# Split weights stored and reloaded through GpSimd's DMA queue in a hybrid decoder step

## The chip, the cores and the metric

One core of a Trainium2 chip runs the whole kernel. The metric is the device time of one launch in microseconds, the median of several runs. The engines are PE (TensorE, matrix products; PEld are its weight loads), DVE (VectorE), ACT (ScalarE), POOL (GpSimd) and SP (SyncE, which here only issues DMA transfers).

## The reference

One layer of a decoder, applied to a prompt of 1024 tokens and to 8 single new tokens with states of their own. Everything is float32, the width D is 1024.

```python
p = jnp.einsum('btd,dn->btn', x, w_in)                  # N_IN = 9360 columns
p_gla, p_rwkv, p_gate = _split(p, (GLA_COLS, RWKV_COLS, GATE_COLS))
# branch 1: gated linear attention, 4 heads, chunked scan over a 128x256 state
o_gla, S_gla = _gla_chunked(q, k, v, log_a, S_gla0)
# branch 2: RWKV-7, 16 heads of 64, token shift, per-token recurrence on a 64x64 state
y, S_rwkv = _rwkv7_scan(rh, w, kh, vh, kk, a, S_rwkv0)
...
m = sigmoid(gate_a) * (o_gla @ w_up_gla) + sigmoid(gate_b) * (o_rwkv @ w_up_rwkv)
y_out = _layernorm(DEEPNORM_ALPHA * x + m @ w_out, ln_g, ln_b, LN_EPS)
```

The outputs are y for both groups, and the new states and shift rows.

## The kernel before, in words

**Tiling and passes.** The tokens are handled in two passes (`PASS`): the first has 512 prompt tokens and the 8 samples (tiles of 256 and 264 columns), the second the other 512 prompt tokens (one tile of 512 columns). In each pass the input projection runs block by block: a block is 128 columns of `w_in` against all 1024 rows, that is 8 steps of 128. When both passes are through the projection, a tail does the two up-projections, the merge, `w_out` and the layer norm.

**Split operands.** For accuracy each float32 operand of the large products is split in a high part, rounded to the format that PE takes at full speed (fp32r), and a low part, the remainder. A product is three matrix products: high x high, high x low, low x high. For a half block of weights (four steps, 128x512) the first pass loads the raw weights into a buffer `wraw` (3 of them), ACT casts the high part into a buffer `wpart` (5 of them, each 128x2x512), and DVE or POOL subtracts to make the low part. The whole `wpart`, 512 KB, is then stored to a scratch tensor `w` in DRAM, `kept[c0, j]`. The second pass needs the same weights: it makes no new split, but loads each stored `wpart` back. There are 73 blocks of `w_in` with two halves each: 146 stores and 146 loads. A buffer `wpart` comes free when PE has done its last product with it. The tail's weights `w_up_gla` and `w_up_rwkv` are split anew, without a store.

**The order of the work.** The kernel's order is not left to a compiler. A planner (class `Order`, method `run`) holds a set of streams, each a generator that yields one operation after the other. At every step it takes, over all streams, the operation that could start first by its own reckoning, corrected by priorities (`PRIO`, `ON_PE`), and emits it. The emitted order is the order of each engine's queue, so what stands first in a queue and waits holds up what stands behind it. To reckon a start the planner keeps `time` for each engine, `ready` and `read` for each tile, `dma` for the time at which the DMA queue will have moved what it was given, and prices from `price` (engine and size) and `transfer` (time in the DMA engines, and a lag until landing). The object `E` stands for operations that DVE or POOL may do (`C` for ACT or DVE): `start` then takes the engine that ends first, with `ASIDE` 0.5 us added where POOL would share its way to memory with DVE.

**Queues.** In the kernel before, every DMA is issued by SP, through one queue. One price holds for each, 0.56 us.

All instructions that the planner emits are recorded at one helper line, L217; tiles tell them apart. `w<-wpart` is a store, `wpart<-w` a load, `wraw<-w_in` a load of raw weights. `proj`, `big`, `pch` and `pY` are PSUM banks, `row`, `wide`, `X`, `XT`, `rh` working tiles, `sg` gate rows kept in DRAM, `XD` and `LD` scratch tensors in DRAM by which small blocks are laid out anew.

Of the kernel before, what the change touches and what calls it, by code (L numbers as in the profile page):

```python
# [10 lines left out]
F32 = mybir.dt.float32  # L11
# [10 lines left out]
D = 1024  # L22
# [107 lines left out]
class Op:  # L130


    def __init__(self, ways, out, ins, lag=0.0, table=None, tiles=None, port=""):
        self.ways, self.out, self.ins, self.lag, self.table, self.tiles = ways, out, ins, lag, table, tiles
        self.port, self.outs = port, [out]
        self.eng, self.fn, self.cost = ways[0]


# [6 lines left out]
def price(eng, name, out, args, ins):  # L145

    n = out.free_size()
    src = [x for x in ins if x.tensor.space != PSUM] if eng == "A" else ins
    if eng == "P":
        m = args[0].free_size()  # L150
        rows, cols = tiles(name, args)
        if name == "transpose":
            return 0.112 * rows / P
        if args[0].dtype == F32R:
            return max(m / 1200, n / 2165)
        if rows == cols == P:
            return 2 * max(m, n) / 1200 + 0.005
        return 2 * (max(m, n) if cols == P else m + n) / 1200 * min(0.5 if cols == P else 0.25, rows * cols / P ** 2) + (0.01 if cols == P else 0.0)
    if eng == "S":
        return 0.56  # L160
    if eng == "A":
        extra = len(ins) - 1
        return 0.097 + n / 1200 + (0.042 if len(src) == len(ins) else 0.0) + 0.094 * extra
    wide = max([n, *(x.free_size() for x in ins)]) if name in ("tensor_reduce", "bn_stats", "bn_aggr") else n
    if eng == "V":
        if name == "tensor_tensor_scan":
            return 0.1 + n / 480
        if name in ("tensor_copy", "copy", "memset") and ins and ins[0].tensor.space != PSUM:
            wide = wide / 2
        scalars = sum(x.free_size() == 1 for x in ins[1:]) if name in ("scalar_tensor_tensor", "tensor_scalar") else 0  # L170
        return 0.068 + wide / (480 if name == "copy_predicated" else 960) + 0.06 * scalars
    if name in ("tensor_scalar", "memset"):
        return 0.08 + n / 760
    return 0.1 + n / (300 if name == "tensor_copy" else 456)
# [31 lines left out]
class Engine:  # L206
# [3 lines left out]
    def __getattr__(self, name):  # L210
        def make(out, *args, **kw):
            ins = [x for x in (*args, *kw.values()) if isinstance(x, AP)]
            ways = []
            lag, table, part, port = 0.0, None, None, ""
            for eng, handle in self._handles.items():
                call = getattr(handle, "tensor_copy" if (eng, name) == ("V", "copy") else name)
                ways.append((eng, lambda call=call: call(out, *args, **kw), price(eng, name, out, args, ins)))  # L217
                if eng in "VG" and shared(eng, name, out, ins):
                    port += eng
            if eng == "S":  # L220
                lag = transfer(out, args[0])
            elif eng == "A" and name == "activation":
                table = SETS.get(args[1])
            elif eng == "P":
                part = tiles(name, args)
            return Op(ways, out, ins, lag, table, part, port)
        return make


# [26 lines left out]
class Order:  # L256
# [4 lines left out]
    def __init__(self, nc):  # L261
        self.P, self.A, self.V, self.G, self.S, self.E, self.C = (Engine(**e) for e in (
            {"P": nc.tensor}, {"A": nc.scalar}, {"V": nc.vector}, {"G": nc.gpsimd}, {"S": nc.sync},
            {"V": nc.vector, "G": nc.gpsimd}, {"A": nc.scalar, "V": nc.vector}))
        self.tiles = (P, P)
        self.quads = {"V": {}, "A": {}}
        self.time = dict.fromkeys("PAVGS", 0.0)
        self.port = dict.fromkeys("VG", 0.0)
        self.dma = 0.0
        self.table = EXP  # L270
        self.ready, self.read = {}, {}
        self.streams = []
        self.idle, self.make, self.home, self.wait = {}, {}, {}, {}
        self.kept, self.tile = {}, {}
# [65 lines left out]
    def start(self, op):  # L340

        best = None
        for eng, fn, cost in op.ways:
            free, t = self.time[eng] + (SWITCH if eng == "P" and op.tiles != self.tiles else 0.0), 0.0
            for x in (*op.outs, *op.ins):
                at, by = self.ready.get(x.tensor.name, (0.0, None))
                if eng == "S" and by == "D" and x is op.out:
                    continue
                if by != eng:
                    at += HOP.get(by, 0.0) + (SPARE if eng == "P" and by in ("V", "A", "G") else LANDED if by == "D" else 0.0)  # L350
                elif eng != "P" and x is not op.out:
                    at += 0.13
                t = max(t, at)
            t = max(t, *(self.read.get(x.tensor.name, 0.0) for x in op.outs))
            if eng in op.port:
                free = max(free, self.port["G" if eng == "V" else "V"])
            late, t = free - t, max(t, free)
            if eng in "VA" and self.held(eng, op):
                cost += HOLD
            end = t + cost  # L360
            if len(op.ways) > 1:
                end += BIAS if eng == "V" and "A" in op.ways[0][0] else ASIDE if eng == "G" and "G" in op.port else 0.0
            if best is None or end < best[0]:
                best = end, t
                op.eng, op.fn, op.cost, op.late = eng, fn, cost, max(0.0, late)
        return best[1]
# [10 lines left out]
    def run(self):  # L377
        while self.streams:
            best, before = None, list(self.streams)
            self.urgent = self.needed()  # L380
            for s in before:
                self.advance(s)
                if s.op is not None:
                    t = self.start(s.op)
                    key = t - (s.on_pe + SWITCH * (s.op.tiles != self.tiles) if s.op.eng == "P" else s.prio)
                    if s.kind in self.urgent:
                        key -= URGENT
                    if s.op.table not in (None, self.table):
                        key += max(0.0, TABLE - AGE * s.op.late)
                    if best is None or key < best[0]:  # L390
                        best = key, t, s
            if best is None:
                assert self.streams != before, "streams wait for one another"
                continue
            _, t, s = best
            op, s.op = s.op, None
            cost = op.cost
            if op.table not in (None, self.table):
                cost += TABLE
                self.table = op.table  # L400
                self.nc.scalar.preload_act_table_set(self.table)  # L401
            op.fn()
            self.time[op.eng] = max(self.time[op.eng], t + cost)
            if op.eng in op.port:
                self.port[op.eng] = t + cost
            if op.eng == "P":
                self.tiles = op.tiles
            elif op.eng in "VA":
                for x, q in self.starts(op):
                    self.quads[op.eng][x is op.out, x.space] = q  # L410
            end = t + cost
            if op.eng == "S":
                self.dma = max(self.dma, end) + op.lag[0]
                end = self.dma + op.lag[1]
            for x in op.outs:
                n = x.tensor.name
                self.ready[n] = max(end, self.ready.get(n, (0.0,))[0]), "D" if op.eng == "S" else op.eng
            for x in op.ins:
                n = x.tensor.name
                self.read[n] = max(self.read.get(n, 0.0), end)  # L420


class Kern(Order):
# [224 lines left out]
    def load_w(self):  # L648
# [16 lines left out]
        def low():  # L665
            for n in range(count):
# [4 lines left out]
                self.free(raw)  # L671
                if src is self.a["w_in"] and i == 0:
                    kept[c0, j] = self.dr.tile([P, 2, 512], F32, name=f"w{c0}_{j}")
                    yield self.S.dma_start(kept[c0, j], w.bitcast(F32))
                self.ws.append(w)
                los.append(w)
            self.w_done = True
# [3 lines left out]
        for n, (src, c0, j, i) in enumerate(todo):  # L681
            if src is self.a["w_in"] and i:
                yield lambda: len(los) == len(raws)
                w = yield from self.get("wpart")
                yield self.S.dma_start(w.bitcast(F32), kept[c0, j])
                self.ws.append(w)
                continue
            raw = yield from self.get("wraw")
# [1151 lines left out]
```

## Time and profile before

| | |
|---|---|
| median of 3 runs | 1487.62 us (1485.31 to 1491.81) |
| the profiled execution's own time | 1487.92 us |
| its span in the profile | 1486.1 us |
| granted TensorE clock, mean | 0.996 |
| PE busy | 1449.8 us (98%) |
| DVE, ACT busy | 1194.8 us (80%), 857.7 us (58%) |
| POOL busy, instructions | 113.6 us (8%), 208 |
| moved by DMA | 318.96 MB, mean 215 GB/s |

The span runs from the first to the last instruction of the kernel; the time of the execution is 1.8 us longer. Busy times leave out the issuing of DMAs. Windows count from the start of the span. In lists of waits a row has the engine and tile that waited, what ended the wait, the total in us, the number of waits and the longest. The first store goes out at 9.1 us and the last at 568.0; the loads run from 568.5 to 1160.2 us.

### The profile page before, as it was taken

The numbers are of one execution on the slowest core, as the hardware profiler recorded it, in microseconds if no ns is written. First come the engines' busy times: TensorE is split into PE (matmuls) and PEld (weight loads), VectorE is DVE, ScalarE is ACT, GpSimd is POOL, SyncE is SP. The second block draws the span as 40 slices with busy tenths as digits, with TensorE's granted clock in tenths as the row PEclk, the third lists the DMA queues.
The fourth block names the chain that finished last, engine by engine and source line by source line (L and its number), as shares of the span: only waits on it lengthen the run. The fifth ranks groups of instructions, "written<-read, shape, count | busy, mean of one in ns | idle before, by whom it ended". The sixth has DMA issues, their size and how long they took to land. (4 is left out here: it accounts for less than half of the span.)

```text
span 1486.1 us, 31563 instructions
## 1 busy us (share of the span) xinstructions
PE 1449.8 (98%) x11158; PEld 1260.4 (85%) x11158; DVE 1194.8 (80%) x3255; ACT 857.7 (58%) x2196; POOL 113.6 (8%) x208
## 2 busy tenths in 40 slices
PE   9999999999999999999999999999999999999997
PEld 6998999899989998787777777878787898988786
DVE  6697889888998899879878989898877866755665
ACT  5666776676767776665754555474547645544210
POOL 1001010201010102000101020111001000000000
PEclk9999999999999999999999999999999999999999
DMA  8886786678676877566566556656564766888432
GB/s 299 273 285 202 250 296 214 226 253 295 202 258 211 294 229 258 170 224 188 160 198 179 155 190 191 192 154 188 174 189 138 229 210 221 295 293 271 139 107 85
DMA packets 211258, 318.96 MB, mean 215 GB/s; under 512 B 91811, under 2 KB 107180, under 8 KB 211100
## 3 DMA queue, kind: packets, MB, share of 16 engines
q1 hardware_dynamic: 211100, 316.93, 66.8%
q8 instruction: 89, 1.46, 0.4%
q14 instruction: 69, 0.57, 0.1%
HBM read 197.19 MB, written 118.61 MB: 212 GB/s over the span
## 5 line engine op out<-in xcount | busy, mean ns | idle before, releaser
L217 PE MATMUL proj<-xs,wpart 128*128 128x264 f32 (+2 forms) x5640 | 1017.7, 327 | 1.4 <-DVE row L217 0.8
L217 PEld LDWEIGHTS proj<-xs,wpart 128*128 128x128 f32 x5640 | 808.5, 189 | 80.3 <-issue 9.9
L217 ACT CAST wpart<-wraw 128x512 fp32r<-128x512 f32 x210 | 130.2, 623 | 103.5 <-PE proj L217 49.6
L217 DVE TENSOR_TENSOR row<-row 128x512 f32<-128x512 f32 (+7 forms) x321 | 166.3, 524 | 12.4 <-ACT row L217 5.6
L217 DVE TENSOR_TENSOR wpart<-wraw,wpart 128x512 fp32r<-128x512 f32 x207 | 145.2, 702 | 32.3 <-ACT wpart L217 31.4
L217 ACT ACTIVATE row<-row 128x512 f32<-128x512 f32 (+5 forms) x213 | 128.8, 610 | 14.4 <-DMA row<-sg 6.5
L217 POOL TENSOR_TENSOR row<-row 128x512 f32<-128x512 f32 (+5 forms) x64 | 72.7, 1143 | 746.3 <-DVE row L217 396.4
L217 DVE TENSOR_TENSOR Xt<-X,wide 128x60 f32<-128x60 f32 (+24 forms) x496 | 104.8, 211 | 11.7 <-DMA wide<-LD 1.8
L217 DVE TENSOR_TENSOR X<-X,Xt 128x60 f32<-128x60 f32 (+24 forms) x496 | 105.4, 213 | 10.0
L217 ACT ACTIVATE row<-proj,omu 128x256 f32<-128x256 f32 (+1 forms) x99 | 54.0, 546 | 93.5 <-PE proj L217 93.3
L217 PE MATMUL big<-xs,wpart 128*128 128x256 f32 (+2 forms) x576 | 101.7, 332 | 0.0
L217 PEld LDWEIGHTS big<-xs,wpart 128*128 128x128 f32 x576 | 87.7, 194 | 9.7 <-issue 0.2
L217 DVE SCALAR_TENSOR_TENSOR wide<-pch,pc,s0p 64x64 f32<-64x64 f32 x208 | 58.7, 282 | 32.9 <-PE pch L217 28.0
L217 ACT COPY row<-wide 64x64 f32<-64x64 f32 x240 | 57.9, 241 | 40.2 <-DVE wide L217 34.7
L401 ACT ACT_TABLE_LOAD x62 | 79.5, 1283 | 1.1
L217 DVE SCALAR_TENSOR_TENSOR row<-proj,pv,row 128x255 f32<-128x255 f32 (+1 forms) x99 | 56.3, 569 | 22.4 <-ACT tail L217 13.7
L217 PE MATMUL big<-row 128*32 128x32 f32 (+4 forms) x936 | 65.3, 241 | 1.4 <-ACT row L217 1.4
L217 ACT COPY row<-big 128x128 f32<-128x128 f32 (+6 forms) x134 | 38.7, 318 | 42.2 <-PE big L217 36.7
L217 ACT COPY wide<-pch 64x64 f32<-64x64 f32 x159 | 32.8, 206 | 47.0 <-PE pch L217 45.1
L217 ACT ACTIVATE row<-proj 128x128 f32<-128x128 f32 (+4 forms) x136 | 36.9, 324 | 37.4 <-PE proj L217 37.0
L217 PE MATMUL pch<-wide,gg 128*128 128x128 f32 x256 | 51.6, 283 | 5.5 <-DVE wide L217 4.7
L217 PEld LDWEIGHTS pch<-wide,gg 128*128 128x128 f32 x256 | 42.3, 189 | 16.1 <-PE proj L217 4.7
(249 smaller groups left out, 1992.6 us busy)
## 6 DMA issues: line engine op xcount, KB each, us to landing
w<-wpart SPq DMA_DIRECT2D x146, 512.0 KB
wpart<-w SPq DMA_DIRECT2D x146, 512.0 KB
wraw<-w_in SPq DMA_DIRECT2D x146, 256.0 KB
wide<-LD SPq DMA_DIRECT2D x64, 128.0 KB
wraw<-w_up_gla SPq DMA_DIRECT2D x32, 256.0 KB
wraw<-w_up_rwkv SPq DMA_DIRECT2D x32, 256.0 KB
sg<-row SPq DMA_DIRECT2D x16, 260.0 KB
row<-sg SPq DMA_DIRECT2D x16, 260.0 KB
```

The source lines that it names most:

```text
L217: ways.append((eng, lambda call=call: call(out, *args, **kw), price(eng, name, out, args, ins)))
L401: self.nc.scalar.preload_act_table_set(self.table)
```

## The change

The stores of `wpart` in the first pass and its loads in the second are issued by POOL (`self.G.dma_start`) instead of SP (`self.S.dma_start`). All other DMAs stay on SP. The planner is told: a DMA on POOL has the price 1.2 us and 1.0 us more until it lands, `dma` is kept for each of the two queues, and what it had tied to the engine SP (`eng == "S"`) is now tied to the operation being a DMA (`op.moves`). As the planner reckons with other prices and two queues, the order that it emits changes on every engine.

```diff
-        self.port, self.outs = port, [out]
+        self.port, self.outs, self.moves = port, [out], False
...
-    if eng == "S":
-        return 0.56
+    if name == "dma_start":
+        return 0.56 if eng == "S" else 1.2
...
-                if eng in "VG" and shared(eng, name, out, ins):
+                if eng in "VG" and name != "dma_start" and shared(eng, name, out, ins):
                     port += eng
-            if eng == "S":
+            if name == "dma_start":
                 lag = transfer(out, args[0])
...
-        self.dma = 0.0
+        self.dma = dict.fromkeys("SG", 0.0)
...
-                if eng == "S" and by == "D" and x is op.out:
+                if op.moves and by == "D" and x is op.out:
                     continue
...
-            if op.eng == "S":
-                self.dma = max(self.dma, end) + op.lag[0]
-                end = self.dma + op.lag[1]
+            if op.moves:
+                self.dma[op.eng] = max(self.dma[op.eng], end) + op.lag[0]
+                end = self.dma[op.eng] + op.lag[1] + (1.0 if op.eng == "G" else 0.0)
...
                     kept[c0, j] = self.dr.tile([P, 2, 512], F32, name=f"w{c0}_{j}")
-                    yield self.S.dma_start(kept[c0, j], w.bitcast(F32))
+                    yield self.G.dma_start(kept[c0, j], w.bitcast(F32))
...
                 w = yield from self.get("wpart")
-                yield self.S.dma_start(w.bitcast(F32), kept[c0, j])
+                yield self.G.dma_start(w.bitcast(F32), kept[c0, j])
```

More of the change, by code (lines that the diff above doesn't have):

```diff
@@ L225, in make @@
                 part = tiles(name, args)
-            return Op(ways, out, ins, lag, table, part, port)
+            op = Op(ways, out, ins, lag, table, part, port)
+            op.moves = name == "dma_start"
+            return op
         return make
@@ L411, in run @@
             end = t + cost
-            if op.eng == "S":
-                self.dma = max(self.dma, end) + op.lag[0]
-                end = self.dma + op.lag[1]
+            if op.moves:
+                self.dma[op.eng] = max(self.dma[op.eng], end) + op.lag[0]
+                end = self.dma[op.eng] + op.lag[1] + (1.0 if op.eng == "G" else 0.0)
             for x in op.outs:
                 n = x.tensor.name
-                self.ready[n] = max(end, self.ready.get(n, (0.0,))[0]), "D" if op.eng == "S" else op.eng
+                self.ready[n] = max(end, self.ready.get(n, (0.0,))[0]), "D" if op.moves else op.eng
             for x in op.ins:
```

## Prediction

> **What bounds the kernel now.** I read the page first (busy shares, then the chain that ended last), then the stages by window, then the lists of waits, and last the rows of the tiles that the change touches.
>
> ```profile
> span 1486.1 us, 31563 instructions
> ...
> PE 1449.8 (98%) x11158; PEld 1260.4 (85%) x11158; DVE 1194.8 (80%) x3255; ACT 857.7 (58%) x2196; POOL 113.6 (8%) x208
> ...
> PE 27%; DMA 2%; DVE 1%; issue 0%; ACT 0%; POOL 0%; SPq 0%; POOLq 0%; DVEq 0%
> ```
>
> PE is busy 1449.8 us of 1486.1, so at most 36.3 us of open idle time can be won without taking work off PE, and the change takes none off. The queues of SP and POOL have 0% of the chain. Some of the 36.3 us is the two ends: the first matmul waits 1.7 us for a memset (row below), and the last stretch of PE in the chain ends at 1475.61 + 2.86 = 1478.5 us, 7.6 us before the end. About 27 us lie between.
>
> ```profile
> 1475.61 2.86 PE big L217 x24
> ```
>
> The stages, with columns span, PE, PEld, DVE, ACT, POOL, granted clock, DMA share and GB/s:
>
> ```profile
> 100.00:200.00 100.00, 96.99 (x886) 90.80 (x886) 82.97 (x238) 67.91 (x188) 6.16 (x12) 1.00 0.75 239
> 200.00:300.00 100.00, 98.23 (x960) 95.16 (x957) 86.49 (x262) 67.98 (x197) 11.71 (x25) 1.00 0.72 234
> 300.00:400.00 100.00, 98.99 (x934) 95.10 (x934) 86.75 (x253) 69.67 (x200) 7.11 (x13) 1.00 0.79 262
> 400.00:500.00 100.00, 96.69 (x962) 91.34 (x960) 90.20 (x245) 72.78 (x197) 12.61 (x26) 1.00 0.73 238
> 500.00:600.00 100.00, 97.96 (x926) 91.25 (x925) 89.44 (x260) 69.46 (x189) 10.10 (x16) 1.00 0.74 243
> 600.00:700.00 100.00, 99.55 (x707) 78.53 (x706) 86.77 (x271) 59.30 (x152) 3.36 (x11) 1.00 0.64 198
> 700.00:800.00 100.00, 97.02 (x628) 77.62 (x627) 79.23 (x214) 59.68 (x145) 12.23 (x20) 1.00 0.58 176
> 800.00:900.00 100.00, 97.09 (x712) 78.39 (x711) 88.76 (x272) 55.18 (x140) 14.60 (x19) 1.00 0.57 175
> 900.00:1000.00 100.00, 98.52 (x671) 77.99 (x670) 89.88 (x251) 58.19 (x143) 15.71 (x22) 1.00 0.61 185
> 1000.00:1100.00 100.00, 99.16 (x608) 80.36 (x606) 79.86 (x226) 51.70 (x139) 8.26 (x18) 1.00 0.63 182
> ```
>
> The reader is to see that PE is near its limit in both passes, that DVE is next with 80 to 90% (86 on the mean of these ten), that the DMA engines have room (0.57 to 0.79), and that POOL is nearly empty. What PE still waits for is DVE above all, and a DMA only once by name:
>
> ```profile
> PEld pch L217 <- DVE rh L217: 6.8, 10, 2.3
> ```
> ```profile
> PE pch L217 <- DVE wide L217: 6.0, 9, 1.7
> PE pch L217 <- DVE rh L217: 4.1, 4, 1.8
> ...
> PE big L217 <- POOL XT L562: 1.7, 1, 1.7
> ...
> PE big L217 <- DMA X<-XD: 1.2, 1, 1.2
> ```
>
> **The change, part by part.** It moves 292 transfers of 512 KB: 146 stores w<-wpart in the first pass and 146 loads wpart<-w in the second. Nothing is removed or added.
>
> ```profile
> L217 SPq DMA_DIRECT2D w<-wpart x146: 319/433/1667, 9.1 to 568.0; - x146
> L217 SPq DMA_DIRECT2D wpart<-w x146: 319/325/597, 568.5 to 1160.2; - x146
> ```
>
> *SP is relieved.* 146 x 0.433 + 146 x 0.325 = 110.7 us of issuing leave it, and with them the waits at its head:
>
> ```profile
> SPq L217 <- PE proj L217: 216.6, 93, 6.9
> ```
>
> This is SP between 570 and 1160 us, where a load waits for PE to be done with a weight buffer, 93 times and 2.3 us on the mean; what is queued behind it waits too. Who gains: the small transfers that others wait for.
>
> ```profile
> DVE X L217 <- DMA XT<-XD: 4.3, 6, 1.3
> ```
> ```profile
> ACT wpart L217 <- DMA wraw<-w_in: 8.7, 8, 2.1
> ACT row L217 <- DMA row<-sg: 6.5, 5, 2.4
> ```
>
> These are engines with idle time of their own, and PE itself waits 1.2 us for a transfer. So the direct gain lies between 0 and the 27 us that PE idles at all; I take 1.5 us, near the 1.2 of PE's own row.
>
> *POOL issues 292 transfers.* No row shows what POOL pays for one. Bounds: SP's 0.32 us from below, and a whole 128x512 operation on POOL from above:
>
> ```profile
> L217 POOL TENSOR_TENSOR row<-row 128x512 f32<-128x512 f32 x36 | 49.1, 1370 | 377.9 <-DVE row L217 141.4 <-ACT row L217 137.4 <-DVE wide L217 75.5
> ```
> ```profile
> L217 POOL TENSOR_TENSOR row<-row 128x512 f32<-128x512 f32 (+5 forms) x64 | 72.7, 1143 | 746.3 <-DVE row L217 396.4
> ```
>
> (The second row is the page's, with all shapes together: POOL has 64 of these in the whole run.)
>
> 292 x 0.32 = 93 us to 292 x 1.37 = 400 us. The planner in the change reckons with 1.2 us, near the upper row, and I take that: 350 us more, so POOL goes from 113.6 to some 464 us, 31% of the span. POOL stays far from being the bound, and this costs nothing by itself.
>
> *POOL's own work is displaced or held up.* The planner may give a tensor operation to DVE or POOL, whichever ends first. With POOL taken 1.2 us in every 4 (1160.2 - 568.5 over 145 loads is 4.08 us a load; 568.0 - 9.1 over 145 stores is 3.85), about 30% of POOL's 64, some 19, go to DVE at about 0.69 us (the median of DVE's subtraction, row below): 13 us more on DVE. DVE idles about 14% of these stages, some 165 us of 1180, so its slack shrinks by nearly a tenth. PE's three largest named waits for DVE, above, sum to 16.9 us; with the small ones I reckon 30 us, and a tenth of them is 3 us. The bounds are 0 (none is moved) and 13 us (all of it falls on PE). Then the order on POOL is fixed: a load that waits 2.3 us for PE now holds POOL's later operations. 93 x 2.3 = 217 us of waiting over 592 us means that about a third of the second pass's POOL operations, 11 if it has half of the 64, are late by a microsecond or two. Their readers are DVE and ACT. I take 1 us on PE for that; bounds 0 and 11 x 2.3 = 25 us.
>
> *The transfers themselves start later.* One more microsecond or two from POOL. The cover in the second pass: five weight buffers, a load each 4.08 us, and the load goes out as PE leaves the buffer, so 5 x 4.08 - 4.08 = 16 us pass from issue to first use. The nearest durations of loads are two of the chain,
>
> ```profile
> 1157.14 4.47 DMA row<-o_gla
> 1161.62 8.32 DMA wraw<-w_up_gla
> ```
>
> of 260 and 256 KB. The larger of them, 1.4 us more for the second 256 KB (at the 182 GB/s of that stage), and 1.2 us of POOL's make 11 us, and 5 us of the cover are left. In the first pass the store must have read its buffer before PE's last use of it frees it. Buffers come free by PE:
>
> ```profile
> ACT wpart L217 <- PE proj L217: 49.6, 48, 3.7
> ```
>
> A buffer is refilled each 5 x 3.85 = 19.3 us; the cast and the subtraction ahead of the store, under a microsecond each, and their hand-overs leave some 16 us for it. Hidden, so 0 us; if POOL were held up for more than those 5 us at a load, the excess would be paid by PE in full.
>
> *The order written for all engines changes.* The planner prices every step and a price has changed, so other neighbours arise everywhere. PE's idle time in the ten windows above runs from 0.45 to 3.31 us, with a mean of 2.0 and a spread of 1.0. Twelve such stages drawn anew spread by 1.0 x 3.5 = 3.5 us; stalls that lie within modelled matmul ends may double that, an estimate, to some 7 us. I take 0 for its mean. The model of queued transfers is also split in two, so that a small load is reckoned to land without the 512 KB ones ahead of it, while all still share the DMA engines; that can only make PE's plan a little too early. It is in the spread.
>
> Sum: -1.5 + 0 + 3 + 1 + 0 + 0 = +2.5 us on the profiled execution's 1487.9, which is 0.3 above the median of the runs (1487.6): 1490 us. What can be told from no change here is about 0.5%, 7.4 us. My own range of the forecast is 1481 to 1495.
>
> **Rivals.**
> *Slower: GpSimd's issuing holds DVE up.* DVE and POOL do get in each other's way in this trace. Beside each other, POOL's and DVE's rows of one moment:
>
> ```profile
> 274.38 1.27 POOL L217 TENSOR_TENSOR wpart<-wraw,wpart 128x512 fp32r<-128x512 f32 x1
> ```
> ```profile
> 274.71 1.49 DVE L217 TENSOR_TENSOR wpart<-wraw,wpart 128x512 fp32r<-128x512 f32 x1
> ```
> ```profile
> L217 DVE TENSOR_TENSOR wpart<-wraw,wpart x207: 648/685/1798, 5.9 to 1368.6; 128x512 fp32r<-128x512 f32 x104
> ```
>
> The DVE operation, 0.685 us at the median, ends just after POOL's and takes 0.8 us longer. If issuing a transfer takes POOL 1.2 us and holds DVE as that does, each of the 292 costs DVE up to 0.8 us, 234 us in all, and DVE with 165 us of idle time becomes the bound: up to 1560 us. With a third of that, 78 us, DVE's idle time halves and PE's waits for DVE about double, by some 25 us: 1513. It decides from about 25 us on DVE, 0.09 us a transfer. Against it: issuing moves no tensor through POOL, and no row shows such a hold.
> The Trainium skill, "SBUF — State Buffer", section "Who interferes with whom", says that DVE and GpSimd share one pair of ports, that the one that starts first keeps it for its whole instruction, and that two-input DVE operations clash only with GpSimd work that reads SBUF, which writing descriptors is inferred not to do. The overlap at 274 us agrees with the first half; by the second half the rival would cost nothing, and no run so far shows it.
>
> *Slower: POOL as a blocked queue.* The bound of 25 us above taken at a half: loads that wait for PE hold POOL operations that DVE needs within a microsecond, and stores that wait for a late subtraction do the same in the first pass: +12 us, 1500. For it: the 93 waits. Against: POOL's 8%, and that its operations are ones the planner found to be spare.
>
> *Faster: SP's head was the brake.* If the 93 waits and the traffic of 512 KB transfers in one row delay the small transfers by more than the named waits show, PE's idle 27 us and its hidden stalls shrink: half of the idle time gone is 1487.9 - 13 = 1475. For it: SP's waits; against: one wait of 1.2 us of PE on a DMA.
>
> **How the numbers follow.** Forecast (within 0.5%, 1481 to 1495) 0.47; SP's head the brake, or a lucky order, 0.22, around 1475; POOL as a blocked queue, or an unlucky order, 0.17, around 1500; DVE held up 0.14, around 1513 and up. The range that leaves out no more than 2 in 10 reaches down to 1474 and up to 1515, the end left open being the far half of the DVE case. Faster by over 0.5% 0.22, within it 0.47, slower 0.31.
>
> **What would show it.** Right: PE's busy time within 3 us of 1449.8 and its idle time 30 to 45 us; POOL with 292 issues, no wait of PE or PEld for wpart<-w beyond a few us in all; DVE's busy time 1195 to 1225; the median of DVE's subtraction still near 685 ns; SP's waits for PE proj nearly gone and found on POOL. Wrong: DVE's rows of unchanged shape longer on the mean (the port), ACT's cast waiting for w<-wpart (stores late), PE waiting for wpart<-w (loads late), POOL's waits followed by DVE waiting for POOL rows (the blocked queue), or waits for XT<-XD, row<-sg and wraw<-w_in all gone with PE's idle time under 25 us (SP was the brake).

## The result and the profile after

The changed kernel takes 1502.98 us at the median of 4 runs (1496.02 to 1505.7), the kernel before 1486.69 us: a ratio of 1.0094 (95% interval 1.0070 to 1.0119), slower by 0.94%. This ratio and those below are estimated from all fast executions of both kernels together, a few disturbed ones left out, so they differ a little from the quotient of the medians (1.0110 here). The execution that was profiled took 1496.02 us, the fastest of the four, so its trace shows 8.1 us of loss against the 1487.92 us of before, and the median some 7 us more, of which there is no trace.

The page of the changed kernel: the span, busy times, DMA queues, the shares of the chain, and the groups of POOL's issues and of one kind of DVE work.

```profile
span 1494.3 us, 31702 instructions
...
PE 1450.3 (97%) x11158; PEld 1261.7 (84%) x11158; DVE 1202.7 (80%) x3309; ACT 849.2 (57%) x2192; POOL 229.4 (15%) x446
...
q1 hardware_dynamic: 169052, 163.82, 37.1%
q0 software_dynamic: 42048, 153.11, 29.6%
...
PE 69%; DVE 13%; DMA 11%; SPq 3%; issue 2%; ACT 2%; POOL 0%; DVEq 0%; POOLq 0%; ACTq 0%
...
L217 DVE TENSOR_TENSOR row<-row 128x512 f32<-128x512 f32 (+8 forms) x355 | 184.7, 528 | 9.9 <-ACT row L217 4.3
...
L217 POOL DMA_DIRECT2D w<-wpart x146 | 78.8, 540 | 458.8 <-DVE wpart L217 186.0
L217 POOL DMA_DIRECT2D wpart<-w x146 | 79.7, 546 | 448.9 <-PE proj L217 367.9
```

PE has the same work (1450.3 against 1449.8 us busy) and 44.0 us of idle time in place of 36.3: over the whole span the loss is idle PE. The traffic is the same, now in two queues that take 37.1 and 29.6% of the same 16 DMA engines, where the one queue of before took 66.8%. The chain's shares can't be set beside those of before, whose chain was followed back only over the last third of the span. POOL pays 0.54 us for an issue; unlike SP's, these 292 issues count in POOL's busy time, with 158.5 of its 229.4 us. DVE has 34 more operations of the kind row<-row than before (355 against 321), 18 us.

The moved transfers, with the time from issue to landing in the last line:

```profile
L217 POOL DMA_DIRECT2D w<-wpart x146: 531/531/767, 6.7 to 579.7; - x146
L217 POOL DMA_DIRECT2D wpart<-w x146: 537/538/612, 581.7 to 1173.1; - x146
...
DMA to landing us min/median/max: 3.0/4.2/8.9
```

The first load goes out at 581.7 us in place of 568.5: the first pass has lost 13 us. The second pass, from the first load to the last, takes 591 us, as before, and what follows the last load is 5 us shorter (321 against 326). So in this trace the whole loss lies in the first pass.

Who waits, in the same lists as before: PE, then DVE, then SP, then all engines.

```profile
PE pch L217 <- DVE rh L217: 6.0, 8, 1.3
PE big L217 <- DVE part L217: 5.8, 5, 2.4
PE big L217 <- DMA X<-XD: 5.1, 4, 2.4
PE pch L217 <- DVE wide L217: 4.1, 4, 2.3
...
PE big L217 <- POOL row L217: 0.9, 1, 0.9
```
```profile
DVE Xt L217 <- DMA wide<-LD: 9.4, 10, 1.9
DVE X L217 <- DMA XT<-XD: 7.0, 8, 1.9
```
```profile
SPq L217 <- ACT row L217: 162.9, 37, 14.3
```
```profile
POOL wpart L217 <- PE proj L217: 367.9, 124, 9.9
```

The waits for PE to leave a weight buffer have moved from SP to POOL, as they should. Nobody waits for w or wpart to land. What has grown is the wait for transfers that stayed on SP, the *small* ones above all: wide<-LD 9.4 us (1.8 before), XT<-XD 7.0 (4.3), X<-XD 5.1 on PE itself (1.2). The row of before for wide<-LD is:

```profile
DVE Xt L217 <- DMA wide<-LD: 1.8, 2, 1.0
```

### The profile page after: what moved, and what is told of

Same layout as the page of the kernel before. It is cut to its first block, busy times and chain, and to the rows that moved or that the text cites. A ratio compares the mean times of both kernels' runs of the same rounds, so it can differ in the third digit from the quotient of the medians.

```text
span 1494.3 us, 31702 instructions
## 1 busy us (share of the span) xinstructions
PE 1450.3 (97%) x11158; PEld 1261.7 (84%) x11158; DVE 1202.7 (80%) x3309; ACT 849.2 (57%) x2192; POOL 229.4 (15%) x446
## 3 DMA queue, kind: packets, MB, share of 16 engines
q1 hardware_dynamic: 169052, 163.82, 37.1%
q0 software_dynamic: 42048, 153.11, 29.6%
## 4 chain that ended last, share of the span: by engine, by line
PE 69%; DVE 13%; DMA 11%; SPq 3%; issue 2%; ACT 2%; POOL 0%; DVEq 0%; POOLq 0%; ACTq 0%
PE proj L217 41%; PE big L217 19%; PE pch L217 5%; DVE row L217 5%; PE pY L217 3%; SPq L217 3%; DMA wide<-LD 2%; DVE X L217 1%; DVE wpart L217 1%; DVE Xt L217 1%; DMA X<-XD 1%; DMA XT<-XD 1%; ACT row L217 1%; DMA wraw<-w_up_gla 1%; DMA row<-state_rwkv 1%
## 5 line engine op out<-in xcount | busy, mean ns | idle before, releaser
L217 DVE TENSOR_TENSOR row<-row 128x512 f32<-128x512 f32 (+8 forms) x355 | 184.7, 528 | 9.9 <-ACT row L217 4.3
L217 POOL DMA_DIRECT2D w<-wpart x146 | 78.8, 540 | 458.8 <-DVE wpart L217 186.0
L217 POOL DMA_DIRECT2D wpart<-w x146 | 79.7, 546 | 448.9 <-PE proj L217 367.9
L217 ACT ACTIVATE row<-row 128x512 f32<-128x512 f32 (+5 forms) x213 | 128.3, 609 | 31.6 <-DVE row L217 13.5
L217 DVE TENSOR_TENSOR Xt<-X,wide 128x60 f32<-128x60 f32 (+24 forms) x496 | 103.8, 209 | 20.1 <-DMA wide<-LD 9.4
L217 PE MATMUL big<-xs,wpart 128*128 128x512 f32 (+2 forms) x576 | 100.4, 328 | 1.0 <-DVE xs L217 0.9
L217 PE MATMUL pch<-rh,XT 128*128 128x128 f32 x256 | 51.1, 281 | 6.0 <-DVE rh L217 6.0
```

## The experiments

The change does two things at once: it moves transfers to another queue, and it makes the planner draw another order. The first four kernels take these apart; all ratios are against the kernel before on the same chip.

**The old order, through POOL's queue.** In the kernel before, the 292 transfers are reckoned as SP's and issued by GpSimd:

```diff
+        self.W = Engine(S=nc.gpsimd)
-  yield self.S.dma_start(kept[c0, j], w.bitcast(F32))
+  yield self.W.dma_start(kept[c0, j], w.bitcast(F32))
-  yield self.S.dma_start(w.bitcast(F32), kept[c0, j])
+  yield self.W.dma_start(w.bitcast(F32), kept[c0, j])
```

> The planner is that of before, so every engine's order is that of before; only the 292 stores and loads of split weights go out through POOL's queue in place of SP's, at the places that the planner gave them. Theory ORDER (the loss comes from the changed order): within 0.4% of before, 1481 to 1493. Theory QUEUES (small transfers now share the DMA engines packet by packet with the 512 KB ones and land later, while the order hardly matters): slower by 0.6 to 1.2%, 1496 to 1505, with DVE and PE waiting longer for wide<-LD, XT<-XD and X<-XD. Theory POOL BLOCKED (POOL's own operations stand behind a transfer that waits): slower by 0.3% or more, with DVE and ACT waiting for POOL rows, more than the before's few.

Measured 1.0038 (1.0024 to 1.0053). The queue alone costs 0.4% in this order, less than half of the loss: just inside the bound of ORDER, and under the range of QUEUES. Its lists for DVE and PE:

```profile
DVE Xt L217 <- DMA wide<-LD: 2.8, 2, 1.9
DVE X L217 <- DMA XT<-XD: 1.4, 2, 1.1
```
```profile
PE big L217 <- DVE part L217: 7.0, 6, 2.2
...
PE big L217 <- DMA X<-XD: 3.3, 2, 2.3
```

The waits for wide<-LD and XT<-XD stay small with the old order (4.2 us together, 6.1 before), so the new queue by itself does not make them. Apart from the memset at the start, all that waits for work of POOL's on another engine is one operation of DVE, for 0.8 us: POOL as a blocked queue falls. Where the 0.4% lies is not settled; PE's wait for DVE part has grown by 4 us and that for X<-XD by 2.

**The new order, through SP's queue.** The changed kernel with `self.W = Engine(G=nc.sync)` for the same two lines: reckoned as in the change, issued by SP.

> The planner is that of after, with its prices, its two reckoned queues and so its order, but the 292 transfers go out through SP's queue. Theory ORDER: as slow as after, ratio 1.007 to 1.012. Theory QUEUES: back to before, 1483 to 1492. POOL BLOCKED: back to before too, or between.

Measured 1.0247 (1.0228 to 1.0266), *slower* than the change itself, which neither theory had. The new order is bad, and POOL's queue softens it.

```profile
DVE Xt L217 <- DMA wide<-LD: 17.9, 9, 3.5
DVE X L217 <- DMA XT<-XD: 13.7, 11, 2.5
```

The small loads are waited for 31.6 us. So it is the new order that asks for them too early; the wait is longest where they stand behind the 512 KB ones in one queue.

**One half of the transfers each.** The changed kernel with the stores back on `self.S`, and with the loads back on `self.S`:

> Only the second pass's 146 loads go through POOL; the stores are SP's and the plan is made anew for that. Theory QUEUES: the loss in proportion to the half that is moved, ratio 1.003 to 1.007, and the first pass like before (first load near 568 us). Theory ORDER: any value from 0.997 to 1.012, since the plan is another one, not tied to the half moved.

> Only the first pass's 146 stores go through POOL, the loads are SP's again. Theory QUEUES: with the loads-only kernel it adds up to after's 1.0094, so 1.003 to 1.007, the loss lying ahead of the first load. Theory ORDER: any value from 0.997 to 1.012, and no adding up.

Loads only 1.0036 (1.0021 to 1.0051), stores only 1.0053 (1.0038 to 1.0069); they add up to 1.0089, nearly the 1.0094. In the kernel with the loads alone, and then in that with the stores alone:

```profile
L217 SPq DMA_DIRECT2D w<-wpart x146: 319/436/1482, 9.1 to 568.8; - x146
L217 POOL DMA_DIRECT2D wpart<-w x146: 527/530/762, 564.0 to 1173.6; - x146
```
```profile
L217 POOL DMA_DIRECT2D w<-wpart x146: 531/531/752, 6.7 to 583.0; - x146
L217 SPq DMA_DIRECT2D wpart<-w x146: 319/320/1387, 584.3 to 1173.1; - x146
```

Each loses in the pass whose transfers it moved: with the loads, 610 us pass from the first load to the last in place of 592; with the stores, the first load is at 584.3 in place of 568.5. That speaks for a systematic cause, with a reserve: the changed kernel, which moves the loads too, lost nothing between its first load and its last. Since both are reckoned with the split model, this does not yet tell queue from order.

**Is any new order worse?** The kernel before, all on SP, with one number of the planner changed (0.56 to 0.55, and to 0.58). Compared line by line, the traces' lists of PE's products differ from that of before in 3536 lines for the first of these and in 4198 for the change itself: the order is redrawn nearly as far.

> The kernel before, all transfers on SP, with one digit of the planner changed: a DMA on SP is reckoned at 0.55 us instead of 0.56. No work and no queue differs, only the order. Theory DRAW (any order drawn anew from this planner is some tenths of a per cent slower than this one, whatever the change is for): slower than before, ratio 1.002 to 1.010, with as many lines of PE's order changed as by the change itself. Theory MODEL (the loss of the new order comes from what it reckons wrongly about the two queues): within 0.3% of before.

> As the run before, with 0.58 us. DRAW: another value from 1.002 to 1.010, not the same as at 0.55 and not in proportion to the step. MODEL: within 0.3% of before.

Measured 0.9972 (0.9951 to 0.9992) and 0.9983 (0.9967 to 1.0000): both a little *faster*. The theory that any new draw is slower expected 1.002 to 1.010 and falls: two redraws differ by 0.2 and 0.3% from before, not by 0.9%. That the change was one unlucky draw is not yet excluded.

**What the new order reckons wrongly.** (The expectations call this theory MODEL, and RECKONING in the last four runs.) The change keeps a time for each queue, as if each had the DMA engines to itself. One edit to the changed kernel gives both one time again, and everything else stays, POOL's queue too:

```diff
-  self.dma[op.eng] = max(self.dma[op.eng], end) + op.lag[0]
-  end = self.dma[op.eng] + op.lag[1] + (1.0 if op.eng == "G" else 0.0)
+  self.dma["S"] = max(self.dma["S"], end) + op.lag[0]
+  end = self.dma["S"] + op.lag[1] + (1.0 if op.eng == "G" else 0.0)
```

> The changed kernel with one edit: the planner reckons all transfers, SP's and POOL's, as moved one after the other, as the DMA engines are shared. MODEL: most of the order's loss of 0.56% is won back, ratio 1.002 to 1.005, and the waits for XT<-XD, wide<-LD and X<-XD shrink. DRAW: somewhere from 1.004 to 1.014, the queue's own 0.38% and a new draw.

Measured 0.9976 (0.9955 to 0.9997): the whole loss is gone, and more. This is better than the model's theory asked (1.002 to 1.005), and outside what DRAW gave (1.004 to 1.014). Its list for DVE:

```profile
DVE Xt L217 <- DMA wide<-LD: 0.7, 2, 0.5
...
DVE S L217 <- DMA XT<-XD: 0.6, 1, 0.6
```

The 16.4 us of waits have become 1.3. The other suspect in the planner is the price of POOL's issue, reckoned at 1.2 us and measured at 0.54. With the two queues still apart, `1.2` became `0.55` and the `1.0` of the landing `0.5`:

> The changed kernel with POOL's DMA reckoned as the trace shows it: 0.55 us of POOL instead of 1.2, and 0.5 us more until landing instead of 1.0. MODEL: ratio 1.002 to 1.006, since POOL gets back its tensor operations (36 of 128x512 row<-row before, 22 after the change). DRAW: somewhere from 1.004 to 1.014.

Measured 1.0054 (1.0035 to 1.0074), with 8.6 us of waits for wide<-LD and 6.9 for XT<-XD. Some of the loss goes, the waits stay.

**Drawn again on both sides.** To tell the reckoning from luck, each side once more with SP's price at 0.58; then the good order on SP's queue; then one reckoned queue with the measured price.

> The changed kernel, its two queues reckoned apart as in the change, with SP's price 0.58 instead of 0.56, so that the order is drawn anew. Theory RECKONING (two queues reckoned as if each had the DMA engines to itself make the plan expect small loads too early): again slow, ratio 1.005 to 1.013, with DVE waiting 5 us or more for wide<-LD and for XT<-XD together. Theory DRAW (the change was an unlucky order): anywhere from 0.996 to 1.010, with even odds of being under 1.003.

> The kernel with one reckoned queue for both, with SP's price 0.58: the same redraw on the other side. RECKONING: again at or under before, ratio 0.994 to 1.001, with small waits for wide<-LD and XT<-XD (under 4 us together). DRAW: anywhere from 0.996 to 1.010.

> The order of the kernel with one reckoned queue, but the 292 transfers go out through SP's queue. If POOL's queue is worth something where the order fits it, this is slower than that kernel's 0.9976, by 0.3% or more: 1.001 to 1.010, with SP waiting for PE again and small loads behind the 512 KB ones. If the queue is worth nothing and all lies in the reckoning, it stays within 0.2% of it: 0.996 to 0.9995.

> One reckoned queue, and POOL's DMA at the measured 0.55 us and 0.5 us more. RECKONING: ratio 0.993 to 1.000; a small gain over the 0.9976 if the overpriced POOL sent work to DVE that POOL could do (the price alone had moved 1.0094 to 1.0054). DRAW: 0.996 to 1.010.

| plan | queue of the 292 | ratio (95%) |
|---|---|---|
| queues reckoned apart, SP 0.58 | POOL | 1.0065 (1.0045 to 1.0084) |
| one reckoned queue, SP 0.58 | POOL | 0.9944 (0.9932 to 0.9955) |
| one reckoned queue | SP | 0.9986 (0.9975 to 0.9997) |
| one reckoned queue, measured price | POOL | 0.9956 (0.9942 to 0.9971) |

The lists for DVE of the first two, in this order:

```profile
DVE X L217 <- DMA XT<-XD: 9.4, 7, 2.7
DVE Xt L217 <- DMA wide<-LD: 8.3, 6, 2.0
```
```profile
DVE X L217 <- DMA XT<-XD: 2.4, 2, 2.1
DVE Xt L217 <- DMA wide<-LD: 2.0, 3, 1.1
...
DVE row L217 <- DMA wide<-LD: 0.4, 1, 0.4
```

All six kernels planned with the queues reckoned apart are slower than before (1.0036 to 1.0247), all six newly planned with a single reckoned queue are faster (0.9944 to 0.9986, one interval reaching 1.0000); as one order of each kind was run on both queues, these are five orders against five. In three pairs only the reckoning differs, and each time it is worth 1.0 to 1.2%: 1.0094 and 0.9976, 1.0065 and 0.9944, 1.0054 and 0.9956. Two of the good ones lie below the least that DRAW gave, 0.996.

The waits for wide<-LD and XT<-XD alone do not sort the kernels. The second of these lists, 4.8 us, is over the bound of 4 us that was set for it; the kernel with the measured price has 6.5 us of them, in a profiled execution of 1488.73 us that was the slowest of its five; before has 6.1; and the kernel with the loads alone has only 6.7 and is slow. Added up over all transfers that DVE and PE wait for (the rows `DVE ... <- DMA` and `PE ... <- DMA` of a trace), the waits do sort them: 19.9 to 56.7 us in the six reckoned apart, 1.5 to 11.7 in the six with one queue, 10.0 before.

The fastest kernel of the study is that with one reckoned queue, POOL's queue and SP's price at 0.58: 1478.75 us, 0.56% under before. How much of that is owed to the queue is open. In the same order POOL's queue against SP's is 0.9976 against 0.9986, with overlapping intervals; in the order of before it is 1.0038 against 1.

## Why the prediction was right or wrong

The measured 1502.98 us lies in the range of 1474 to 1515, and slower had 31%, but the forecast of no change, 1490 us, did not come true, and none of the rivals named the cause that the runs showed. That the range holds the time is owed to rivals that were wrong. The signs given for being right were nearly all there in the trace (PE's busy time, 44.0 us of idle time, DVE's 1202.7 us, no wait for wpart<-w, SP's waits moved to POOL): none of them watched for small loads that come too late.

**The step that failed** is that of the order: "I take 0 for its mean", and of the split model "that can only make PE's plan a little too early. It is in the spread". It is no spread but a bias. With POOL's queue in both, the order reckoned apart costs 1.0094 and that reckoned together 0.9976: 1.2%, about 17 us, in the term that was set to 0. In the trace of the change DVE waits 10 us longer than before for wide<-LD and XT<-XD, and PE 4 us longer for X<-XD.

The 13 us of the first pass can be followed further. PE has three gaps there, of 3.19, 2.39 and 2.37 us, that end at 18.26, 178.95 and 573.49 us; in the first pass of before none is over 1.73 us. The chain that the profile infers goes back in each to a load on SP (start, duration, load), and around the first and the last of them, as around the second (last section), PE has half its clock (the column after POOL):

```profile
12.74 4.38 DMA row<-gla_alpha_w
...
170.60 5.42 DMA row<-vd
...
568.13 5.11 DMA X<-XD
```
```profile
19.60:23.05 3.45, 3.45 (x18) 3.45 (x18) 1.61 (x5) 1.61 (x3) 1.05 (x2) 0.51 0.96 353
572.50:579.40 6.90, 5.91 (x114) 3.90 (x114) 4.74 (x12) 2.16 (x6) 0.40 (x1) 0.51 0.41 157
```

The gaps are 8.0 us; the three slow stretches, 13.7 us at half clock, lose some 6.8 more, an estimate. Before has no slow stretch in its first pass. By the windows of the two first passes PE idles 20.1 us in place of 13.0 and is busy 561.6 in place of 555.5, which makes up the 13 us. The 7 us by which the median lies above the profiled execution are not followed: there the granted clock was 0.993, 0.993 and 0.989, against 0.994 in the trace and 0.996 before, so slow stretches may well be a part of them.

The spread itself was put at 7 us; the redraws on SP moved by 2.5 and 4.2 us.

**The price of POOL's issue** was put at 1.2 us between 0.32 and 1.37; it is 0.54, nearer to SP's row than to POOL's tensor work. POOL went to 229 us, not 464: 158.5 us of issues, and 71 us of its own work in place of 114. Whether it costs nothing by itself is open: in the old order POOL's queue costs 0.4%, in the order with one reckoned queue nothing that can be told.

**Displaced work** was put at 19 operations and 13 us on DVE; by the rows row<-row it is 34 and 18 us (POOL has 30 left of 64). DVE's busy time rose by 7.9 us (1194.8 to 1202.7), in the band given. That this costs PE 3 us could not be told apart from the rest. The 16.9 us of waits that it was worked out from count one stall twice, as they add PEld's wait for rh to PE's: PE alone has 10.1 us in these rows.

**The transfers start later, and are hidden:** right. They land in 4.2 us at the median and 8.9 at most, inside the 16 us of cover, and no one waits for them.

**SP relieved:** the direct gain was put at 1.5 us; in the old order, relieving SP of 292 issues brought no gain but a loss of 0.4%, so SP's head was not the brake in that order.

**DVE held up by GpSimd's issuing:** not borne out, by the row of the changed kernel that answers to 648/685/1798:

```profile
L217 DVE TENSOR_TENSOR wpart<-wraw,wpart x209: 664/685/695, 5.6 to 1376.9; 128x512 fp32r<-128x512 f32 x105
```

146 stores are issued among these operations and none is longer than 695 ns. The 16 of them that overlap an issue are few, but nine do so for over 0.3 us and take 685 ns on the mean, those that overlap none 686. That agrees with what "SBUF — State Buffer" in the Trainium skill infers in "Who interferes with whom", that writing descriptors does not clash with two-input work on DVE.

**POOL as a blocked queue:** it had nearly the right time, 1500, for the wrong reason. POOL does stand waiting for PE (367.9 us), but DVE, ACT and PE together wait under 4 us for work of POOL's after the start, and with the old order the same queue made DVE wait 0.8 us and PE not at all.

## What to carry to other kernels

Moving transfers to a second queue did not give them DMA engines of their own here: the two queues took 37.1 and 29.6% of the 16 engines, where the one took 66.8%. Where a plan of the work is made from reckoned landing times, the second queue must draw on the same budget, or, as here, work that depends on small loads is put too early; one edit that restored the common budget won the whole loss back. "DMA: Bandwidth & Descriptors" in the Trainium skill says, under "Issuing engines are not separate DMA queues", that DMAs run on the same 16 engines and interleave, whichever engine issued them. The two shares and the edit agree with that. And where a change also redraws an order, run the old order with the new resource, the new order with the old one, and a redraw that changes nothing else, before any of the time is ascribed to the resource.

## What the runs showed of the hardware that was not expected

A gap on PE can cost more than its length. Around the second-longest gap of the changed kernel, PE's row of the timeline, and two windows with the granted clock in the column after POOL:

```profile
178.95 0.50 PE L217 MATMUL big<-part,headsr 128*128 128x512 f32 x1 [2.39 <-DVE part L217]
```
```profile
176.50:180.10 3.60, 1.21 (x8) 1.06 (x8) 2.92 (x8) 3.60 (x10) 0.00 (x0) 1.00 0.99 348
180.10:183.50 3.40, 3.40 (x18) 3.40 (x17) 3.40 (x6) 3.06 (x9) 0.65 (x2) 0.50 0.58 177
183.50:186.90 3.40, 3.40 (x32) 2.85 (x32) 1.59 (x3) 2.89 (x7) 0.53 (x1) 1.00 0.69 207
```

After 2.39 us without work PE has half its clock (0.50) for 3.4 us: 18 products in that window and 32 in the next, some 1.7 us lost on top of the gap, an estimate, in a stretch that counts as fully busy. Not every gap does this: after one of 2.32 us that ends at 1184.24 us in the same trace the clock stays at 1.00. "TensorE: Matmul & The Clock Gate" in the Trainium skill, "Part 1: The HAM clock gate", has the clock fall to half after an idle window of about 3.4 us. In this trace the length of the slow stretch agrees; an idle stretch of 2.39 us was enough.
